# Turning the residual stream to tokens on VectorE and through DRAM instead of on TensorE

## The chip, the core and the metric

The kernel runs on one core of a Trainium2 chip. The metric is the device time of one execution in microseconds (us); the figure to be predicted is the median over several runs. The engines are named as in the profile: PE is TensorE (PEld its weight loads), DVE is VectorE, ACT is ScalarE, POOL is GpSimd and SP is SyncE, which here only issues DMAs. Each engine works through its own instructions in a fixed order and waits for others by semaphores. TensorE's granted clock is the full 2.4 GHz in nearly the whole trace.

## The reference

Two layers of a decoder trunk on 256 tokens of width 1024, in float32. Each layer adds four things to the residual stream `x`, and a last norm follows:

```
x += 1/2 SwiGLU(RMSNorm x)                       # ffn1
x += mixer(RMSNorm x)                            # layer 0: short conv | sliding-window attention; layer 1: block-sparse attention
x += MemoryCrossAttn(RMSNorm x, RMSNorm mem)
x += 1/2 SwiGLU(RMSNorm x)                       # ffn2
out = RMSNorm(x)                                 # after the last layer
SwiGLU(h) = (silu(h @ w_gate) * (h @ w_up)) @ w_down      # 1024 -> 2816 -> 1024
RMSNorm(x) = x * rsqrt(mean(x*x) + 1e-6) * g
```

## The kernel before

The stream is kept with the features on the partitions: `x` is a tile of 128 partitions by 8 feature blocks by 256 tokens. Every weight tile of 128 x 128 is loaded by SP from one long stream in DRAM, in chunks of 16 tiles (1 MB), and split into a high and a low part: ACT rounds it to `whi` (L128), DVE forms the rest `wlo` (L129). A block of 8 tiles is split at a time; splitting runs up to four blocks ahead of their use, in five buffers. For one tile TensorE does two matmuls into an accumulator (L385 with `whi` on 512 columns, L386 with `wlo` on 256). Four PSUM banks named `acc` hold accumulators.

A product of 8 such tiles makes one group: 128 features of a gate or of an up projection. When a group is done, `join` copies its PSUM bank into a `w1` tile (L395 on ACT, L396 on DVE; eight `w1` buffers). When gate and up of one `f` are both there, and the norm's factor is known, `evac` multiplies, applies silu, and splits the result for the down projection (L513, L514, L516, L453, L454).

The norm's factor may come late, since the matmuls use `x` times the gain, and the factor 1/rms per token is multiplied in afterwards. Its way is a chain over all engines. POOL squares the feature blocks and adds them up as they are made (`squares`: L325, L329, L330); for the last block ACT squares (L332, into the one `sq` buffer that POOL used) and DVE adds (L333). TensorE sums over the partitions (L354), DVE scales (L356), POOL takes the power -1/2 (L358, `rcol`), TensorE spreads the result over the partitions (L364), ACT copies it out (L366, `rbc`). Until `rbc` is there no `evac` can run; groups that finish before it wait in their `w1` tiles and then in their PSUM banks.

The last ffn differs at its end: its down projection is made with the tokens on the partitions, so that the result can be normalized and stored as it is. For that `x` must be turned as well, into `xtok` (its SBUF buffer is named `bias`). That is `to_tokens`, called 20 us into this ffn: 16 transposes on TensorE (L476), in four PSUM tiles, each copied out by ACT (L477). `xtok` is first read when the left half of the down projection is done (L571), near 938 us of the span.

The order in which an engine meets its instructions is set in two steps: a small planner in the kernel calls the pieces by due times and costs, and a scheduler of the language then orders the instructions by a simulated timeline, so an instruction that waits long in that simulation may stand later in its engine's order.

Of the kernel before, what the change touches and what calls it, by code (L numbers as in the profile page):

```python
# [15 lines left out]
F32 = mybir.dt.float32  # L16
F32R = mybir.dt.float32r
AF = mybir.ActivationFunctionType
# [5 lines left out]
P = 128  # L24
D = 1024
KT = D // P
S = 256
# [216 lines left out]
def build(nc, tc, ctx, a):  # L244
    consts = ctx.enter_context(tc.tile_pool(name="consts", bufs=1))
    wpool = ctx.enter_context(tc.tile_pool(name="wpool", bufs=1))
    act = ctx.enter_context(tc.tile_pool(name="act", bufs=1))
    psum = ctx.enter_context(tc.tile_pool(name="psum", bufs=1, space=PSUM))
    dram = ctx.enter_context(tc.tile_pool(name="dram", bufs=1, space=DRAM))
# [7 lines left out]
    def tr_tile():  # L257
        return psum.tile([P, 512], F32, name="tr", bufs=2)
# [11 lines left out]
    x = consts.tile([P, KT, S], F32, name="x")  # L270
# [8 lines left out]
    ident = consts.tile([P, P], F32, name="ident")  # L279
# [8 lines left out]
    pt = tr_tile()  # L288
# [3 lines left out]
    pe = Order()  # L292
# [175 lines left out]
            nc.vector.tensor_tensor(lo, src, hi.bitcast(F32), op=ALU.subtract)  # L468

    def to_tokens(out):  # L470
        def go():
            for u in range(2):
                for c in range(2):
                    pt = tr_tile()
                    for k in range(4):
                        nc.tensor.transpose(pt[:, k * P:(k + 1) * P], x[:, 4 * c + k, u * P:(u + 1) * P], ident)  # L476
                    nc.scalar.activation(out[:, u, c * 512:(c + 1) * 512], pt, AF.Copy)  # L477
        return go


    def ffn(which, layer, n, nxt, first=False, last=False):
# [39 lines left out]
        def down(j):  # L521
            def go():
                ps = acc_tile()
                ws.fine = j == KT - 1
                for k in range(FT):
                    w = ws.take(f"{which}_w_down", layer, k * P, j * P)
                    (mm_narrow if ws.fine else mm)(ps, w, h[k], k == 0, k == FT - 1)
                t = w1()
                part = unpaired(ps[:, :S]) if ws.fine else halves(join(t, ps))
                nc.vector.scalar_tensor_tensor(halves(t), part, 0.5, halves(n.rbc), op0=ALU.mult, op1=ALU.mult)  # L530
                add_to_x(j, halves(t), nxt)
                ws.flush()

            return always, go, FT * 327
# [66 lines left out]
        if last:  # L601
            xtok = act.tile([P, 2, D], F32, name="bias", bufs=1)
            gfin = act.tile([P, D], F32, name="kT", bufs=1)
            src = a["final_norm"]
            nc.sync.dma_start(gfin, bass.AP(tensor=src.tensor, offset=src.offset, ap=[[0, P], [1, D]]))
            pe.after(20000, to_tokens(xtok), 2000)
        pe.run(ups + (down_tok() if last else [down(j) for j in range(KT)]))


# [485 lines left out]
    pe.after(30000, biases, 0)  # L1095
    pe.after(60000, mem_scale, 0)
    ffn("ffn1", 0, n, nxt, first=True)
    bias, sinks = early["bias"], (vecs[:, VCOL["sinks"]:VCOL["sinks"] + 8], nsinks)

# [12 lines left out]
    bias = load_bias(1)  # L1112
    n, nxt = nxt, xn(("ffn1_norm", 1))
    ffn("ffn2", 0, n, nxt)
    n, nxt = nxt, xn(("mix_norm", 1))
    ffn("ffn1", 1, n, nxt)
    n, nxt = nxt, xn(("xa_norm", 1))
    odd_mixer(n, nxt, bias, mem_keys(1))
# [75 lines left out]
```

## Time and profile before

| | |
|---|---|
| median of 3 runs | 976.91 us (976.83 to 977.02) |
| the profiled execution | 975.91 us |
| its span in the profile | 974.1 us |
| PE, DVE, ACT, POOL busy | 965.1, 771.9, 599.7, 137.4 us |
| moved by DMA | 194.73 MB, 200 GB/s |

The span is the time from the first to the last instruction that the profiler shows; the execution is 1.8 us longer. Matmuls overlap each other, so a row's duration is longer than what the matmul adds to TensorE's time: that is read from the starts of neighbouring rows. Times of the rows below are from the span's start.

### The profile page before, as it was taken

To read this page: it belongs to the slowest core of one execution; us is meant where nothing else is said; L and a number is where in the kernel's file an instruction comes from. 1 tells how busy PE (TensorE), PEld (TensorE's weight loads), DVE (VectorE), ACT (ScalarE), POOL (GpSimd) and SP (SyncE) were. 2 spreads that over 40 slices of the span, in tenths; PEclk is the share of its full clock that TensorE was granted. 3 is DMA by queue.
4 is the path that set the end of the run, shared out by engine and by line. 5 is a ranking of instruction groups with operands and counts; after the bars stand their busy time and mean duration, and the time that the engine had idled before them with its cause. 6 is when DMAs were issued, how large, how long until landed. Compare 5 with 4: busy or idle time off the path is not lost.

```text
span 974.1 us, 16976 instructions
## 1 busy us (share of the span) xinstructions
PE 965.1 (99%) x6576; PEld 903.8 (93%) x6576; DVE 771.9 (79%) x1319; ACT 599.7 (62%) x1106; POOL 137.4 (14%) x149
## 2 busy tenths in 40 slices
PE   9999999999999999999999999999999999999997
PEld 8899999999999899999999999999999999999896
DVE  6989777798878987877878788777878798887663
ACT  7666655696666766665556666556784768666541
POOL 3114012201232200002300000221005050000011
PEclk9999999999999999999999999999999999999999
DMA  9896566455545666556555565565644346665631
GB/s 356 293 352 245 193 211 204 169 191 194 185 141 190 215 205 212 193 197 210 193 202 200 194 212 192 197 214 177 229 155 167 127 168 222 211 202 193 211 131 43
DMA packets 28496, 194.73 MB, mean 200 GB/s; under 512 B 3298, under 2 KB 3938, under 8 KB 5760
## 3 DMA queue, kind: packets, MB, share of 16 engines
q1 hardware_dynamic: 27072, 187.84, 55.5%
q0 software_dynamic: 912, 5.37, 1.6%
q8 instruction: 51, 0.84, 0.3%
q10 hardware_dynamic: 432, 0.44, 0.1%
q14 instruction: 29, 0.24, 0.1%
HBM read 192.57 MB, written 4.22 MB: 202 GB/s over the span
## 4 chain that ended last, share of the span: by engine, by line
PE 93%; DVE 3%; DMA 1%; ACT 1%; issue 1%; SPq 0%; POOLq 0%; DVEq 0%
PE acc L385 40%; PE acc L386 20%; PE acc L390 7%; PE acc L392 7%; PE acc L391 7%; DVE wlo L129 2%; PE acc L562 1%; PE acc L561 1%; PE acc L560 1%; DMA raw<-in_w 1%; DVE x L318 1%; PE acc L898 1%; PE acc L897 1%; PE acc L899 1%; DVE x L448 1%
## 5 line engine op out<-in xcount | busy, mean ns | idle before, releaser
L129 DVE TENSOR_TENSOR wlo<-raw,whi 128x1024 fp32r<-128x1024 f32 (+2 forms) x375 | 439.2, 1174 | 140.6 <-ACT whi L128 137.7
L128 ACT ACTIVATE whi<-raw 128x1024 fp32r<-128x1024 f32 (+2 forms) x375 | 369.7, 990 | 282.3 <-PE acc L385 134.3
L385 PE MATMUL acc<-x,whi 128*128 128x512 f32 x1392 | 458.4, 383 | 0.9 <-ACT whi L128 0.6
L386 PE MATMUL acc<-x,wlo 128*128 128x256 f32 x1392 | 378.0, 273 | 0.6 <-DVE wlo L129 0.5
L385 PEld LDWEIGHTS acc<-x,whi 128*128 128x128 f32 x1392 | 262.5, 189 | 38.4 <-ACT whi L128 1.0
L386 PEld LDWEIGHTS acc<-x,wlo 128*128 128x128 f32 x1392 | 267.3, 192 | 2.3 <-DVE wlo L129 1.5
L385 PE MATMUL acc<-h,whi 128*128 128x512 f32 x462 | 151.3, 382 | 0.0
L386 PE MATMUL acc<-h,wlo 128*128 128x256 f32 x462 | 125.4, 273 | 0.0
L385 PEld LDWEIGHTS acc<-h,whi 128*128 128x128 f32 x462 | 87.1, 189 | 12.0
L386 PEld LDWEIGHTS acc<-h,wlo 128*128 128x128 f32 x462 | 88.7, 192 | 0.2
L391 PE MATMUL acc<-h,whi 128*128 128x256 f32 x322 | 87.8, 276 | 0.0
L392 PE MATMUL acc<-h,wlo 128*128 128x256 f32 x322 | 87.7, 275 | 0.0
L390 PE MATMUL acc<-h,whi 128*128 128x256 f32 x322 | 86.5, 276 | 0.0
L391 PE MATMUL acc<-x,whi 128*128 128x256 f32 x304 | 84.1, 278 | 0.0
L392 PE MATMUL acc<-x,wlo 128*128 128x256 f32 x304 | 83.9, 277 | 0.0
L390 PE MATMUL acc<-x,whi 128*128 128x256 f32 x304 | 83.0, 277 | 0.0
L396 DVE TENSOR_TENSOR w<-acc,w 128x256 f32<-128x256 f32 x195 | 81.4, 418 | 1.1 <-ACT w L395 0.7
L395 ACT ACTIVATE w<-acc 128x256 f32<-128x256 f32 x195 | 71.8, 369 | 5.4 <-PE acc L386 5.2
L391 PEld LDWEIGHTS acc<-h,whi 128*128 128x128 f32 x322 | 61.7, 192 | 0.1
L392 PEld LDWEIGHTS acc<-h,wlo 128*128 128x128 f32 x322 | 61.7, 192 | 0.1
L390 PEld LDWEIGHTS acc<-h,whi 128*128 128x128 f32 x322 | 60.6, 192 | 0.4 <-DVE x L448 0.2
L325 POOL TENSOR_TENSOR sqacc<-x 128x256 f32<-128x256 f32 x7 | 4.3, 611 | 395.4 <-DVE x L448 395.4
(209 smaller groups left out, 1304.4 us busy)
## 6 DMA issues: line engine op xcount, KB each, us to landing
raw<-in_w SPq DMA_DIRECT2D x171, 1024.0 KB, 4.9
dists<-line POOLq DMA_DIRECT2D x2, 1536.0 KB, 12.2
raw<-in_memT SPq DMA_DIRECT2D x3, 1024.0 KB, 5.2
raw<-in_w SPq DMA_DIRECT2D x6, 384.0 KB, 6.1
bias<-dists POOLq DMA_DIRECT2D x2, 1024.0 KB, 11.4
x<-in_xT SPq DMA_DIRECT2D x1, 1024.0 KB, 7.6
out<-bias SPq DMA_DIRECT2D x2, 320.0 KB, 2.4
kT<-in_final_norm SPq DMA_DIRECT2D x1, 512.0 KB, 5.7
```

Of the source, the lines that this page charges most:

```text
L128: for ins in (self.nc.scalar.activation(hi[:, at], src, AF.Copy), self.nc.vector.tensor_tensor(lo[:, at], src, hi[:, at].bitcast(F32), op= ...
L129: self.nc.vector.tensor_tensor(lo[:, at], src, hi[:, at].bitcast(F32), op=ALU.subtract)):
L318: nc.vector.scalar_tensor_tensor(x2.lo, halves(src), g, x2.hi.bitcast(F32), op0=ALU.mult, op1=ALU.subtract)
L385: nc.tensor.matmul(ps, w[0], x2.both, start=start, stop=False)
L386: nc.tensor.matmul(ps[:, :S], w[1], x2.high, start=False, stop=stop)
L390: nc.tensor.matmul(ps[:, :S], w[0], x2.high, start=start, stop=False)
L391: nc.tensor.matmul(ps[:, :S], w[0], x2.low, start=False, stop=False)
L392: nc.tensor.matmul(ps[:, :S], w[1], x2.high, start=False, stop=stop)
L395: nc.scalar.activation(halves(out), unpaired(ps[:, S:]), AF.Copy)
L396: nc.vector.tensor_tensor(halves(out), unpaired(ps[:, :S]), halves(out), op=ALU.add)
L448: nc.vector.tensor_tensor(halves(x[:, j]), part, halves(x[:, j]), op=ALU.add)
L560: nc.tensor.matmul(ps, hh, wh, start=f == 0, stop=False)
```

## The change

`to_tokens` no longer uses TensorE and ACT. For each pair of feature blocks DVE turns a tile of 128 x 512 in blocks of 32 by 32 (a block stays at its place, only its inside is transposed). The result goes to DRAM in eight DMAs issued by POOL, each 32 partitions by 256 elements, 32 KB, written as 256 runs of 32 floats (128 bytes), so that the blocks come to their places in an array `tok` of 256 tokens by 1024 features. That makes 32 DMAs of this kind. One more DMA, also on POOL's queue, reads `tok` back into `xtok`. The turned tiles are named `q2` and have two buffers.

```diff
     def to_tokens(out):
-        def go():
-            for u in range(2):
-                for c in range(2):
-                    pt = tr_tile()
-                    for k in range(4):
-                        nc.tensor.transpose(pt[:, k * P:(k + 1) * P], x[:, 4 * c + k, u * P:(u + 1) * P], ident)
-                    nc.scalar.activation(out[:, u, c * 512:(c + 1) * 512], pt, AF.Copy)
-        return go
+        tok = dram.tile([S, D], F32, name="tok")
+        to = tok.rearrange("(c i) (k p j) -> p k i c j", i=32, p=4, j=32)
+        for k in range(0, KT, 2):
+            t = act.tile([P, 2 * S], F32, name="q2", bufs=2)
+            nc.vector.transpose(t, x[:, k:k + 2].rearrange("p k s -> p (k s)"))
+            for p in range(4):
+                for i in range(2):
+                    nc.gpsimd.dma_start(to[p, k + i], t[32 * p:32 * p + 32, i * S:(i + 1) * S].rearrange("i (c j) -> i c j", j=32))
+        nc.gpsimd.dma_start(out, tok.rearrange("(u q) f -> q u f", u=2))
...
-            pe.after(20000, to_tokens(xtok), 2000)
+            pe.after(20000, lambda: to_tokens(xtok), 0)
```

In the changed kernel the lines behind `to_tokens` have numbers three higher; the DVE transposes are L477, the DMAs to `tok` L480, the one back L481.

The engines' orders differ only around the start of the last ffn. POOL's order before, from the squares of the sixth feature block to the norm's factor (`sq` and `sqacc` are the squares and their sum, `rcol` the factor):

```order
L329 TENSOR_TENSOR sq_9484<-x_69 128x256
L330 TENSOR_TENSOR sqacc_9427<-sqacc_9427,sq_9484 128x256
L329 TENSOR_TENSOR sq_9508<-x_69 128x256
L330 TENSOR_TENSOR sqacc_9427<-sqacc_9427,sq_9508 128x256
L329 TENSOR_TENSOR sq_9528<-x_69 128x256
L330 TENSOR_TENSOR sqacc_9427<-sqacc_9427,sq_9528 128x256
L358 TENSOR_TENSOR rcol_9586<-ms_9584,mhalf_97 128x2
```

The same engine and place in the changed kernel, from the third set of eight DMAs (the first two sets stand right above, after the first and the second square):

```order
L480 DMA tok_9795<-q2_9816 32x8x32 x8
L329 TENSOR_TENSOR sq_9462<-x_69 128x256
L480 DMA tok_9795<-q2_9826 32x8x32 x8
L330 TENSOR_TENSOR sqacc_9427<-sqacc_9427,sq_9462 128x256
L329 TENSOR_TENSOR sq_9484<-x_69 128x256
L330 TENSOR_TENSOR sqacc_9427<-sqacc_9427,sq_9484 128x256
L329 TENSOR_TENSOR sq_9508<-x_69 128x256
L330 TENSOR_TENSOR sqacc_9427<-sqacc_9427,sq_9508 128x256
L481 DMA bias_9555<-tok_9795 128x2x1024
L329 TENSOR_TENSOR sq_9528<-x_69 128x256
L330 TENSOR_TENSOR sqacc_9427<-sqacc_9427,sq_9528 128x256
L358 TENSOR_TENSOR rcol_9586<-ms_9584,mhalf_97 128x2
```

All 33 DMAs now stand between the squares, ahead of the last square and of the norm's factor. TensorE's order before, from the sums over partitions (L354) to the spreading (L364) of that norm (`acc` with a number is one group of the last ffn; 9588, 9627 and 9649 are its second, third and fourth):

```order
L354 MATMUL tr_9581<-ones_95,sqacc_9427 128x1 x2
L386 MATMUL acc_9588<-x_9549,wlo_9432 128x256
L385 MATMUL acc_9627<-x_9549,whi_9487 128x512
L386 MATMUL acc_9627<-x_9549,wlo_9488 128x256
L386 MATMUL acc_9649<-x_9481,wlo_9532 128x256
L385 MATMUL acc_9649<-x_9505,whi_9531 128x512
L386 MATMUL acc_9649<-x_9505,wlo_9532 128x256
L385 MATMUL acc_9649<-x_9525,whi_9531 128x512
L386 MATMUL acc_9649<-x_9525,wlo_9532 128x256
L385 MATMUL acc_9649<-x_9549,whi_9531 128x512
L386 MATMUL acc_9649<-x_9549,wlo_9532 128x256
L364 MATMUL tr_9608<-ident_90,rcol_9586 128x128 x2
```

The same place in the changed kernel (9915 is the twelfth group of the last ffn, 9950 its thirteenth):

```order
L386 MATMUL acc_9915<-x_9525,wlo_9789 128x256
L385 MATMUL acc_9915<-x_9549,whi_9788 128x512
L386 MATMUL acc_9915<-x_9549,wlo_9789 128x256
L354 MATMUL tr_9581<-ones_95,sqacc_9427 128x1 x2
L364 MATMUL tr_9608<-ident_90,rcol_9586 128x128 x2
L385 MATMUL acc_9950<-x_9424,whi_9881 128x512
L386 MATMUL acc_9950<-x_9424,wlo_9882 128x256
```

The sums and the spreading have moved behind the twelfth group, eight groups later, and no other work of TensorE stands between them or between the spreading and the thirteenth group.

## Rows read from the trace of the kernel before

**Rows 1.** The page, busy time, share of the span and instructions of engines

```profile
PE 965.1 (99%) x6576; PEld 903.8 (93%) x6576; DVE 771.9 (79%) x1319; ACT 599.7 (62%) x1106; POOL 137.4 (14%) x149
```

**Rows 2.** The page, chain that ended last, by engine

```profile
PE 93%; DVE 3%; DMA 1%; ACT 1%; issue 1%; SPq 0%; POOLq 0%; DVEq 0%
```

**Rows 3.** Timeline of PE, 801 to 817 us: start, duration, instructions

```profile
801.51 0.50 PE L354 MATMUL tr<-ones,sqacc 128*128 128x1 f32 x4
...
803.48 0.38 PE L364 MATMUL tr<-ident,rcol 128*128 128x128 f32 x2
...
804.09 0.48 PE L385 MATMUL acc<-x,whi 128*128 128x512 f32 x1
...
804.51 0.38 PE L385 MATMUL acc<-x,whi 128*128 128x512 f32 x1
...
804.84 0.38 PE L385 MATMUL acc<-x,whi 128*128 128x512 f32 x1
...
815.10 1.04 PE L476 MATMUL tr<-ident,x 128*128 128x128 f32 x8
815.90 0.46 PE L385 MATMUL acc<-x,whi 128*128 128x512 f32 x1
```

**Rows 4.** Timeline of POOL, 786 to 803 us

```profile
786.43 0.61 POOL L325 TENSOR_TENSOR sqacc<-x 128x256 f32<-128x256 f32 x1 [29.22 <-DVE x L448]
...
797.73 1.59 POOL L330 TENSOR_TENSOR sqacc<-sqacc,sq 128x256 f32<-128x256 f32 x1
802.28 0.70 POOL L358 TENSOR_TENSOR rcol<-ms,mhalf 128x2 f32<-128x2 f32 x1 [2.96 <-DVE ms L356]
```

**Rows 5.** Groups of POOL's instructions: busy us, mean ns, idle before

```profile
L852 POOL DMA_DIRECT2D bias<-dists x2 | 1.9, 939 | 34.4 <-PE tr L713 27.0 <-PE acc L386 7.5
L845 POOL DMA_DIRECT2D dists<-line x2 | 1.1, 546 | 1.9 <-DMA line<-kT 1.9
...
L843 POOL DMA_DIRECT2D line<-kT x1 | 0.6, 644 | 10.4 <-DVE kT L842 10.4
```

**Rows 6.** DMA issues: KB each, median us from issue to landing

```profile
dists<-line POOLq DMA_DIRECT2D x2, 1536.0 KB, 12.2
...
bias<-dists POOLq DMA_DIRECT2D x2, 1024.0 KB, 11.4
...
line<-kT POOLq DMA_DIRECT2D x1, 24.0 KB, 2.2
```

**Rows 7.** Timeline of DVE, 781 to 804 us

```profile
781.45 0.69 DVE L129 TENSOR_TENSOR wlo<-raw,whi 128x512 fp32r<-128x512 f32 x1
...
800.73 0.41 DVE L333 TENSOR_TENSOR sqacc<-sqacc,sq 128x256 f32<-128x256 f32 x1
802.04 0.16 DVE L356 TENSOR_SCALAR ms<-tr 128x2 f32<-128x2 f32 x1 [0.91 <-PE tr L354]
...
803.61 0.42 DVE L396 TENSOR_TENSOR w<-acc,w 128x256 f32<-128x256 f32 x1
```

**Rows 8.** Chain that ended last, in order of time: start, us, what

```profile
797.18 3.22 DVE wlo L129 x2
```

**Rows 9.** Timeline of ACT, 799 to 813 us

```profile
799.36 0.42 ACT L332 ACTIVATE sq<-x 128x256 f32<-128x256 f32 x1 [2.18 <-POOL sqacc L330]
...
806.24 0.40 ACT L366 ACTIVATE rbc<-tr 128x256 f32<-128x256 f32 x1
...
808.37 1.28 ACT L514 ACT_TABLE_LOAD   x1
809.66 0.72 ACT L514 ACTIVATE w<-w 128x256 f32<-128x256 f32 x2
...
811.24 0.36 ACT L395 ACTIVATE w<-acc 128x256 f32<-128x256 f32 x1
...
811.98 0.72 ACT L453 ACTIVATE h<-w 128x256 fp32r<-128x256 f32 x2
```

## The prediction

> **What bounds the kernel now.** I read the page first: TensorE is busy for 99% of the span, DVE for 79%, POOL for 14% [rows 1], and the chain that ended last runs on PE for 93% of its length [rows 2]. So what counts is whether TensorE is kept going, and what of its own work goes. POOL's low share says little: around a norm, POOL is a link in a chain that TensorE waits for. That chain is read from four timelines of the same 20 us. POOL starts the last norm's squares at 786.43 and ends its last sum at 797.73 + 1.59 = 799.32 [rows 4]; ACT squares the last block at once, at 799.36 [rows 9]; DVE adds it at 800.73 [rows 7]; TensorE sums at 801.51 and spreads the factor at 803.48 [rows 3]. TensorE loses almost nothing there, because in its order ten matmuls of the second to fourth group lie between the sums and the spreading, and behind them banks are free.
>
> **The change part by part.**
>
> *Removed from TensorE:* eight transposes take from 815.10 to 815.90, 0.10 us each [rows 3]; 16 of them are 1.6 us, all on the path. The four ACT copies go too; ACT is not the bound, so I count nothing for them.
>
> *Added on DVE:* four transposes of 128 x 512. The trace has none; the nearest row is a DVE pass of the same shape, 0.69 us [rows 7]. At nothing the term would be 0, at twice the row 2.8 us in all; I take 0.6 us each. The first two stand among the adds to `x`, where DVE itself is on the chain for stretches (two splits, 3.22 us, at 797.18 [rows 8]), so 1.2 us reach TensorE. The third and fourth stand between joins, where DVE has room; they also wait for the eight DMAs that empty their buffer. Behind them in DVE's order are weight splits and joins. By the count below those DMAs are issued about when DVE gets there, and splits lie up to four blocks ahead, so I price this at nothing; without that cover it would add the wait's length.
>
> *Moved on TensorE:* sums and spreading stand behind the twelfth group instead of among the first four. A tile's pair takes 804.84 - 804.51 = 0.33 us, a group of eight pairs 2.62 us [rows 3]. The fifth group began at 804.09 after four transposes (0.4), the spreading (0.2) and the sums (0.4) that are no longer ahead of it, so it begins near 803.1; eight groups end at 803.1 + 21.0 = 824.1, with DVE's 1.2 us at 825.3. Before, the thirteenth group began at 804.09 + 21.0 + 12 x 0.10 = 826.3.
>
> *Added on POOL, ahead of the norm's factor:* 33 DMA issues. In the changed order they stand between the squares; the last square, hence the factor, is behind all of them. POOL's own DMAs cost 0.546 us (128 plain rows), 0.644 us (24 KB in a three-dimensional pattern) and 0.939 us (1024 runs) per issue [rows 5]. The new ones have 256 runs in such a pattern, between the last two. I take the middle, 0.79 us, and keep 0.55 and 0.94 as ends by these rows. 32 x 0.79 = 25.3 us; the one that reads back has 256 rows and gets 0.9 us. Added to 799.32 this gives the last sum at 825.5 (818 to 830.4). Landing should not hold POOL up: a queue slot comes round after eight DMAs, 6.3 us, and 24 KB landed in 2.2 us [rows 6]; the read-back waits for all 32 but has three sums and two squares ahead of it.
>
> *The restart.* From there to the sums: ACT 0.42, DVE 0.41 [rows 9, 7] and the hand-overs, 1.3 us: 826.8, later than TensorE's own 825.3. Now the chain is bare, since nothing stands between: sums to factor done 802.28 + 0.70 - 801.51 = 1.5 us, to the spreading 0.5 [rows 3, 4], then `rbc` (0.4 from spreading to its start, 0.40 long), the table load of 1.28 that stands behind it, four silus at 0.36, one split of `h` at 0.36, the copy of the ninth group's bank 0.36 [rows 9] and its DVE add 0.42 [rows 7], because all eight `w1` tiles and all four banks are full: in sum 6.7 us, and 0.1 to TensorE. The thirteenth group begins at 826.8 + 6.8 = 833.6. The next three banks follow within a group's time each, and up to four blocks of weights lie split, so I count no second stop.
>
> *Sum:* 833.6 - 826.3 = +7.3 us (the 1.6 us saved is in both numbers: 1.2 in the second, 0.4 in the first). The profiled execution's 975.91 becomes 983.2. It lies 1.0 us under the median of the runs, 976.91, which becomes 984.2; I say 984. With the ends of the issue price: at 0.55 TensorE's own 825.3 decides and the sum is +5.8 us, 982.7; at 0.94 it is +12.1 us, 989.
>
> **The rivals.**
>
> *Landing decides, not issue.* The third set needs buffers that the first set must have left, and a slot takes its next DMA when its last one has landed. The row that speaks for it is 1 MB in 1024 runs, 11.4 us to land [rows 6]; against it, 24 KB took 2.2 us. At 11.4 us the sets go out every 11.4: the last issue near 788.4 + 3 x 11.4 + 6.3 = 828.9, landed at 840.3, then the read-back's issue and a square and a sum (0.9 + 2.3): 843.5. With 1.3 + 6.8 us the thirteenth group begins at 851.6, +25 us: 1002. DVE's fourth transpose would then wait near 807 to 817 for the second set, inside the same stop. The weight stream shares the engines meanwhile; its chunks are three ahead.
>
> *Each DMA waits for the one ahead.* If POOL were held until a DMA has landed, 32 x 2.2 us = 70 us [rows 6] would stand in POOL's order instead of 25.3, and the last sum would be at 870.6: +52 us, 1029. Against it: two DMAs of 12.2 us each had 1.9 us of idle time before both together [rows 5, 6], so the second did not wait for the first. The Trainium skill, "DMA: Bandwidth & Descriptors", section "Anatomy of one DMA — SWDGE (gpsimd) path", gives such a DMA about 2.0 us fixed plus its bytes over 436 GB/s, and says elsewhere that transfers under 64 KB are mostly overhead; 32 x 2.1 us would be an estimate of 67 us if none overlapped. By that rule, taken one by one, the time would be near this rival's; the 2.2 us row agrees with its fixed part, and the back-to-back issues show that it overlaps.
>
> *Not slower.* TensorE's 16 transposes go, DVE and POOL have idle time, and the norm's chain ends before the twelfth group does. For this the issues must cost 0.7 us or less and also the bare restart of 6.8 us must be gone, for instance because the waiting banks are emptied in another order than L516, silu and L453 come. Then only -1.6 + 1.2 us are left: 976.5; with DVE's part hidden 975.3. Against it stands TensorE's order: nothing lies between sums, spreading and the thirteenth group, and no bank is free. It decides only below 1.6 us of restart.
>
> **How the numbers follow.** The forecast (+5.8 to +12, issue-bound) gets 0.62, landing 0.24, one by one 0.06, not slower 0.05, and 0.03 is left for stops that I don't see. About 0.2% is what a measurement here can tell from no change. Faster by that takes the second form of the last rival and more, 0.02; within it 0.04; slower 0.94. The forecast's own range is 981 to 990. The range to be held 8 times in 10 starts at 980 and reaches up through most of the landing case, to 1004.
>
> **What the profile would show.** Right: no L476 on PE; POOL busy without gaps from 786 to about 825 with L480 rows of 0.6 to 0.95 us; one stop of PE near 825, of 7 to 10 us, ending at the first matmul of the thirteenth group, released by DVE's L396; nothing changed after 840 but the shift. Landing would show as idle POOL time between sets with a DMA as releaser, and a PE stop over 20 us. One by one would show such gaps before every issue. I am wrong if PE has no stop over 3 us in 800 to 850, or if a second stop, from late splits or late weight chunks, is as long as the first.

## The result and the profile after

| | before | after |
|---|---|---|
| median, lowest to highest | 976.96 us (976.83 to 978.19) | 988.40 us (987.04 to 989.28), 4 runs each |
| ratio, 95% interval | | 1.0118 (1.0105 to 1.0130) |
| the profiled execution, its span | 975.91, 974.1 us | 989.16, 987.0 us |

The change makes the kernel 11.4 us slower. The forecast was 984, so the sign and the stop were foreseen and the size was 4.4 us short.

Before the two traces are compared, one offset has to be taken out. The first square of the last norm stands at 786.43 before [rows 4] and at 788.75 after, 2.3 us later, although no changed instruction runs ahead of it. The delay is older still: the first weight load for a norm's sums stands at 27.5 us before and at 29.8 after (all instructions of one line, in the traces of before and of after: durations, then first and last start):

```profile
L354 PEld LDWEIGHTS tr<-ones,sqacc x36: 189/192/192, 27.5 to 801.7; 128*128 128x128 f32 x36
L354 PEld LDWEIGHTS tr<-ones,sqacc x36: 189/192/333, 29.8 to 831.1; 128*128 128x128 f32 x36
```

It arises in the first 9 us. TensorE waits there 2.39 us for a weight split, where it waited 0.56 us before, and that split waits 2.24 us for its weights to land, 0.36 us before. So below, "in before's time" means 2.3 us less than the trace of after shows. TensorE's page row and its timeline around the last norm (start, duration, instructions, idle time before and what ended it):

```profile
PE 966.0 (98%) x6560; PEld 903.5 (92%) x6560; DVE 771.9 (78%) x1323; ACT 598.5 (61%) x1102; POOL 156.6 (16%) x182
```

```profile
804.82 0.27 PE L386 MATMUL acc<-x,wlo 128*128 128x256 f32 x1
806.75 0.48 PE L385 MATMUL acc<-x,whi 128*128 128x512 f32 x1 [1.65 <-DVE w L396]
...
827.70 0.27 PE L386 MATMUL acc<-x,wlo 128*128 128x256 f32 x1
830.60 0.95 PE L354 MATMUL tr<-ones,sqacc 128*128 128x1 f32 x4 [2.63 <-DVE sqacc L333]
832.59 0.69 PE L364 MATMUL tr<-ident,rcol 128*128 128x128 f32 x2 [1.04 <-POOL rcol L358]
837.71 0.77 PE L385 MATMUL acc<-x,whi 128*128 128x512 f32 x1 [4.43 <-DVE w L396]
...
838.48 0.63 PE L385 MATMUL acc<-x,whi 128*128 128x512 f32 x1
...
841.00 0.38 PE L385 MATMUL acc<-x,whi 128*128 128x512 f32 x1
...
841.32 0.38 PE L385 MATMUL acc<-x,whi 128*128 128x512 f32 x1
```

Where TensorE went on without a gap before [rows 3], it now stops twice: 1.65 us ahead of the fifth group, and from the end of the twelfth group, 827.97, to the thirteenth at 837.71, a gap of 9.7 us with 0.6 us of necessary work in it. And it comes out of the gap slowly: a tile's pair takes 0.64 us from 838.48 on, twice the 0.33 of before, until 841.00. The stretches around it say why (columns: the stretch, its length, busy time of five engines, granted TensorE clock, DMA share, GB/s):

```profile
824.00:828.00 4.00, 3.97 (x25) 3.39 (x23) 2.20 (x2) 1.16 (x2) 2.15 (x3) 1.00 0.86 317
828.00:832.00 4.00, 0.95 (x4) 0.86 (x4) 1.72 (x3) 1.26 (x2) 0.17 (x1) 0.84 0.99 387
832.00:836.00 4.00, 0.69 (x2) 0.29 (x2) 2.14 (x7) 2.65 (x6) 0.54 (x1) 0.50 0.13 53
836.00:840.00 4.00, 2.29 (x7) 2.05 (x8) 4.00 (x13) 3.07 (x11) 0.00 (x0) 0.50 0.00 0
840.00:844.00 4.00, 4.00 (x23) 3.58 (x23) 2.60 (x6) 2.50 (x5) 0.00 (x0) 0.88 0.00 0
```

With TensorE busy for only 0.95 and 0.69 us of two stretches, its granted clock fell from 1.00 to 0.50, that is to 1.2 GHz. From 837.71 to 841.00 five pairs take 3.29 us; at full clock five such pairs took 0.42 + 4 x 0.33 = 1.74 [rows 3]. That costs 1.55, rounded 1.6 us.

POOL, the engine on which the forecast let the stop depend, first with its timeline, then with all DMAs to `tok` in one row (durations in ns, least, median and most) and their landing:

```profile
788.75 0.61 POOL L325 TENSOR_TENSOR sqacc<-x 128x256 f32<-128x256 f32 x1 [29.22 <-DVE x L448]
...
802.97 4.62 POOL L480 DMA_DIRECT2D tok<-q  x8 [1.20 <-DVE q L477]
...
813.56 4.64 POOL L480 DMA_DIRECT2D tok<-q  x8 [5.26 <-DVE q L477]
...
823.79 0.76 POOL L481 DMA_DIRECT2D bias<-tok  x1
...
825.52 0.73 POOL L330 TENSOR_TENSOR sqacc<-sqacc,sq 128x256 f32<-128x256 f32 x1
```

```profile
L480 POOL DMA_DIRECT2D tok<-q x32: 585/585/642, 790.7 to 817.6; - x32
...
DMA to landing us min/median/max: 1.9/3.2/6.0
```

POOL ends its last sum at 825.52 + 0.73 = 826.25. The sums on TensorE start 4.35 us later. What lies between is on ACT and DVE:

```profile
804.04 1.06 ACT L128 ACTIVATE whi<-raw 128x1024 fp32r<-128x1024 f32 x1 [4.54 <-PE acc L385]
...
827.90 1.06 ACT L128 ACTIVATE whi<-raw 128x1024 fp32r<-128x1024 f32 x1 [1.56 <-PE acc L385]
828.86 0.40 ACT L332 ACTIVATE sq<-x 128x256 f32<-128x256 f32 x1
833.32 0.38 ACT L366 ACTIVATE rbc<-tr 128x256 f32<-128x256 f32 x1 [4.06 <-PE tr L364]
833.72 1.28 ACT L517 ACT_TABLE_LOAD   x1
```

```profile
801.97 0.70 DVE L477 STREAM_TRANSPOSE q<-x 128x512 f32<-128x512 f32 x1
...
828.99 1.23 DVE L129 TENSOR_TENSOR wlo<-raw,whi 128x1024 fp32r<-128x1024 f32 x1 [1.39 <-ACT whi L128]
830.13 0.42 DVE L333 TENSOR_TENSOR sqacc<-sqacc,sq 128x256 f32<-128x256 f32 x1
...
837.15 0.42 DVE L396 TENSOR_TENSOR w<-acc,w 128x256 f32<-128x256 f32 x1
```

The last square (L332) and its sum (L333) stand on their engines behind one block's weight split (L128, L129). That split waits until TensorE, at the end of the twelfth group, lets go of a split buffer. So the norm's last step waits for the very group behind which TensorE then waits for the norm.

In the trace of before the thirteenth group began here:

```profile
826.46 0.38 PE L385 MATMUL acc<-x,whi 128*128 128x512 f32 x1
```

In before's time the step is: thirteenth group at 835.4 against 826.5, +8.9 us; half clock, +1.6; together 10.5. The spans differ by 12.9, without the late start by 10.6.

### The profile page after: what moved, and what is told of

Read it like the earlier page. It is cut to its first block, busy times and chain, and to the rows that moved or that the text cites. A ratio compares the mean times of both kernels' runs of the same rounds, so it can differ in the third digit from the quotient of the medians.

```text
span 987.0 us, 16987 instructions
## 1 busy us (share of the span) xinstructions
PE 966.0 (98%) x6560; PEld 903.5 (92%) x6560; DVE 771.9 (78%) x1323; ACT 598.5 (61%) x1102; POOL 156.6 (16%) x182
## 4 chain that ended last, share of the span: by engine, by line
PE 94%; DVE 2%; ACT 1%; issue 1%; DMA 1%; POOL 0%; SPq 0%; POOLq 0%; DVEq 0%
PE acc L385 40%; PE acc L386 20%; PE acc L392 7%; PE acc L390 7%; PE acc L391 7%; PE acc L565 1%; PE acc L564 1%; PE acc L563 1%; DVE wlo L129 1%; PE acc L901 1%; PE acc L902 1%; PE acc L900 1%; DMA raw<-in_w 1%; ACT whi L128 0%; PE sc L563 0%
## 5 line engine op out<-in xcount | busy, mean ns | idle before, releaser
L129 DVE TENSOR_TENSOR wlo<-raw,whi 128x1024 fp32r<-128x1024 f32 (+2 forms) x375 | 437.0, 1168 | 152.0 <-ACT whi L128 146.8
L128 ACT ACTIVATE whi<-raw 128x1024 fp32r<-128x1024 f32 (+2 forms) x375 | 369.5, 989 | 293.9 <-PE acc L385 148.2
L385 PEld LDWEIGHTS acc<-h,whi 128*128 128x128 f32 x462 | 87.1, 189 | 12.0
L396 DVE TENSOR_TENSOR w<-acc,w 128x256 f32<-128x256 f32 x195 | 81.3, 417 | 1.1 <-ACT w L395 0.7
L391 PEld LDWEIGHTS acc<-h,whi 128*128 128x128 f32 x322 | 61.7, 192 | 0.1
L329 POOL TENSOR_TENSOR sq<-x 128x256 f32<-128x256 f32 x42 | 47.4, 1128 | 88.3 <-DVE x L448 87.2
## 6 DMA issues: line engine op xcount, KB each, us to landing
bias<-dists POOLq DMA_DIRECT2D x2, 1024.0 KB, 11.4
```

What stands on the lines that cost most here:

```text
L128: for ins in (self.nc.scalar.activation(hi[:, at], src, AF.Copy), self.nc.vector.tensor_tensor(lo[:, at], src, hi[:, at].bitcast(F32), op= ...
L129: self.nc.vector.tensor_tensor(lo[:, at], src, hi[:, at].bitcast(F32), op=ALU.subtract)):
L329: nc.gpsimd.tensor_tensor(sq, src, src, op=ALU.mult)
L385: nc.tensor.matmul(ps, w[0], x2.both, start=start, stop=False)
L391: nc.tensor.matmul(ps[:, :S], w[0], x2.low, start=False, stop=False)
L396: nc.vector.tensor_tensor(halves(out), unpaired(ps[:, :S]), halves(out), op=ALU.add)
```

## The experiments

Three theories. A: the loss is made by the place at which sums and spreading stand in TensorE's order; behind the twelfth group nothing covers the norm's chain, whatever POOL's real pace. B: POOL's time for the DMA issues is the loss, since the factor is late by as much as POOL is busy. C: DVE's transposes, and the waits for their two buffers, are the loss. Each kernel is compared with runs of the kernel before on the same chip: their median was 976.09 us (26 runs) for the first four kernels and 976.43 (9 runs) for the other four.

**The turning behind the factor.** Each turned tile first takes a column of the factor, so nothing of the turning can come ahead of the norm. The same transposes and DMAs are made, and one small copy on POOL for each tile.

```diff
-    def to_tokens(out):
+    def to_tokens(out, n):
...
             t = act.tile([P, 2 * S], F32, name="q2", bufs=2)
+            nc.gpsimd.tensor_copy(t[:, :1], n.rcol[:, :1])
             nc.vector.transpose(t, x[:, k:k + 2].rearrange("p k s -> p (k s)"))
```

> All of the change, but each turned tile first gets one element from the norm's factor, so that transposes and DMAs come behind the factor on DVE and POOL; sums and spreading are back among the first four groups in TensorE's order. Theory A (the place of the sums in TensorE's order makes the stop): no stop near 825, 975 to 976 us, the 1.6 us of TensorE's transposes gained less what DVE gives back. Theory B (POOL's time for the DMA issues makes the factor late): the same, since the issues are behind the factor. Theory C (the four transposes and their waits for buffers take DVE from the splits and joins): still slower than before, 979 us or more.

Measured: 974.75 us (974.30 to 975.67), ratio to before 0.9985 (0.9976 to 0.9994). TensorE's sums stand at 801.75 and its spreading at 803.72, as before. The waits of TensorE and of POOL from 784 to 870 us, one row of each (waiter, releaser, us in total, times, longest):

```profile
PE acc L385 <- DVE w L396: 0.2, 1, 0.2
```

```profile
POOL tok L481 <- DVE q L478: 12.3, 3, 5.7
```

All added work is still there, POOL even waits 12.3 us for DVE, and 1.3 us are gained: TensorE's 1.6 for the transposes less 0.2 of a wait. So neither the transposes nor the waits for their buffers cost much where they stand behind the factor; C among the adds to `x` is left to the third experiment. This is the version that beats both kernels.

**The DMAs from SP.** The order of issue is kept, but POOL is freed of it.

```diff
-                    nc.gpsimd.dma_start(to[p, k + i], ...)
-        nc.gpsimd.dma_start(out, ...)
+                    nc.sync.dma_start(to[p, k + i], ...)
+        nc.sync.dma_start(out, ...)
```

> All of the change, but the 33 DMAs are issued by SP instead of POOL, at the same early place; the first two DVE transposes stay among the adds to x. In TensorE's order the sums stand behind the fourth group and the spreading behind the fifth. A: the long stop is gone, 976 to 978 us. B: the same or less, 975 to 977. C: 980 us or more, since the transposes are where they were. A risk outside all three: weight loads stand behind the 32 issues in SP's queue; if they come late, PE waits for splits with a DMA as releaser, some us.

Measured: 976.43 us (976.01 to 978.03), ratio 1.0003 (0.9994 to 1.0012): no difference from before. The sums now stand behind the fourth group and the spreading behind the fifth; TensorE's timeline there:

```profile
803.70 0.50 PE L354 MATMUL tr<-ones,sqacc 128*128 128x1 f32 x4
805.51 0.48 PE L385 MATMUL acc<-x,whi 128*128 128x512 f32 x1 [1.31 <-DVE w L396]
...
808.24 0.38 PE L364 MATMUL tr<-ident,rcol 128*128 128x128 f32 x2
```

The 10 us are gone with POOL's issues; 1.3 us of stop, and 0.3 elsewhere, stay and eat the 1.6 us of the transposes. But this run takes away both POOL's time and the late place, so A and B are not yet told apart.

**DVE's transposes alone.** The kernel before, with the four DVE transposes added and read by nobody; TensorE's transposes stay.

```diff
+    def turn_only():
+        for k in range(0, KT, 2):
+            t = act.tile([P, 2 * S], F32, name="q2", bufs=2)
+            nc.vector.transpose(t, x[:, k:k + 2].rearrange("p k s -> p (k s)"))
...
+            pe.after(20000, turn_only, 0)
             pe.after(20000, to_tokens(xtok), 2000)
```

> The kernel before, with its TensorE transposes, and the four DVE transposes added whose tiles nobody reads; no new DMA. Sums stand behind the fourth group, spreading behind the fifth. A and B: 977 to 979 us, 1 to 2 us for the first two transposes that stand among the adds. C: most of the loss, 983 us or more.

Measured: 978.57 us (977.86 to 979.58), ratio 1.0023 (1.0014 to 1.0033), +2.2 us by the ratio and +2.5 by the medians. TensorE waits 1.3 us for L396 ahead of the fifth group, like the SP kernel, and twice 0.3. So the four transposes, with the order that they bring about, cost 2 to 2.5 us, of which the forecast had 1.2, and C does not make the 11 us.

**The DMAs alone.** The kernel before, with 32 DMAs of the same pattern on POOL, straight from `x` to an array that nobody reads; no DVE transposes and no read-back, and TensorE's transposes stay.

```diff
+    def copy_only():
+        tok = dram.tile([S, D], F32, name="tok")
+        to = tok.rearrange("(c i) (k p j) -> p k i c j", i=32, p=4, j=32)
+        for k in range(0, KT, 2):
+            for p in range(4):
+                for i in range(2):
+                    nc.gpsimd.dma_start(to[p, k + i], x[32 * p:32 * p + 32, k + i].rearrange("i (c j) -> i c j", j=32))
...
+            pe.after(20000, copy_only, 0)
             pe.after(20000, to_tokens(xtok), 2000)
```

> The kernel before, with its TensorE transposes, and the 32 DMAs on POOL straight from x to an array that nobody reads (no DVE transposes, no read-back). In TensorE's order sums and spreading stand behind the twelfth group, as in the changed kernel. A: the same stop, 9 to 11 us at half clock behind it, 985 to 988 us. B: POOL has no waits for DVE here and needs no read-back, its last sum comes 6 to 7 us earlier than in the changed kernel, so the loss should shrink by as much, 980 to 982. C: 977.

Measured: 987.01 us (986.36 to 987.62), ratio 1.0109 (1.0095 to 1.0122). POOL, which never waits for DVE here, then DVE and TensorE:

```profile
796.34 2.88 POOL L486 DMA_DIRECT2D tok<-x  x5 [0.79 <-DMA tok<-x]
...
820.15 0.73 POOL L330 TENSOR_TENSOR sqacc<-sqacc,sq 128x256 f32<-128x256 f32 x1
828.42 0.71 POOL L358 TENSOR_TENSOR rcol<-ms,mhalf 128x2 f32<-128x2 f32 x1 [7.54 <-DVE ms L356]
```

```profile
825.92 1.22 DVE L129 TENSOR_TENSOR wlo<-raw,whi 128x1024 fp32r<-128x1024 f32 x1 [1.39 <-ACT whi L128]
827.06 0.42 DVE L333 TENSOR_TENSOR sqacc<-sqacc,sq 128x256 f32<-128x256 f32 x1
```

```profile
824.63 0.27 PE L386 MATMUL acc<-x,wlo 128*128 128x256 f32 x1
827.53 0.61 PE L354 MATMUL tr<-ones,sqacc 128*128 128x1 f32 x4 [2.63 <-DVE sqacc L333]
...
834.23 0.66 PE L476 MATMUL tr<-ident,x 128*128 128x128 f32 x4 [1.84 <-ACT bias L477]
835.66 0.80 PE L385 MATMUL acc<-x,whi 128*128 128x512 f32 x1 [0.78 <-DVE w L396]
```

This run tells A from B. POOL is done at 820.88, 4.0 us before the twelfth group ends at 824.90, and TensorE still waits 2.63 us for L333, to the hundredth as in the changed kernel, and again begins the thirteenth group only at 835.7. The square and its sum wait for the split behind the twelfth group, not for POOL. The stop is there without a single DVE transpose.

**The changed kernel once more.** Unchanged, beside the three kernels that follow.

> The changed kernel itself again, beside the next three on one chip and in more runs: its profiled run began its first layer 2.3 us later than that of before, which the change has no part in. If that was this one run's start, the median here lies 10.5 to 11 us above before, 986.5 to 987.5; if the start is always late, 988 or more.

Measured: 987.38 us (986.40 to 988.62), ratio 1.0113 (1.0099 to 1.0127), +10.95 us. The profiled execution, 988.62, shows the same stops (1.65, 2.63, 1.05 and 4.43 us) and a start 1.5 us late (its first square of the last norm at 787.91). Without their late starts the two profiled executions of this kernel would take 986.9 and 987.1 us. One thing differs: seven slow pairs follow the stop here, from the first row to the second, and not five.

```profile
836.53 0.77 PE L385 MATMUL acc<-x,whi 128*128 128x512 f32 x1 [4.43 <-DVE w L396]
...
841.14 0.38 PE L385 MATMUL acc<-x,whi 128*128 128x512 f32 x1
```

They take 4.61 us; seven at full clock would take 0.42 + 6 x 0.33 = 2.40, so the clock cost 2.2 us in this execution.

**The stop filled.** Matmuls with zeros keep TensorE at work in the stop: 10 into the open accumulator of the twelfth group, 16 into the spreading's bank once `rbc` is copied out.

```diff
             nc.scalar.activation(n.rbc, pt[:, :S], AF.Copy)
+            if n.last:
+                for _ in range(16):
+                    nc.tensor.matmul(pt[:, :P], warm, warm, start=True, stop=True)
...
+                if last and f == 5 and part == 1 and ks[-1] == KT - 1:
+                    for i in range(10):
+                        nc.tensor.matmul(ps[:, :P], warm, warm, start=False, stop=i == 9)
...
```

> The changed kernel with TensorE work of no use put into its stop: 10 matmuls of a zero tile into the open accumulator of the twelfth group ahead of the sums (about 2.3 us), 16 into the spread factor's PSUM tile once it is read (about 3.8 us). Nothing waits less. If the half clock behind the stop costs the 1.6 us that its slow matmuls show (five tile pairs of 0.64 us instead of 0.33), the time falls by 1 to 2 us against the changed kernel on this chip; if the stop alone is the price, it stays within 0.4 us; if the filling is itself late, it rises by 1 or more.

Measured: 985.89 us (985.58 to 986.52), ratio to before 1.0098 (1.0084 to 1.0111). TensorE, with a start 0.1 us late, and the stretches:

```profile
828.36 0.61 PE L355 MATMUL tr<-ones,sqacc 128*128 128x1 f32 x4 [0.40 <-DVE sqacc L334]
...
830.92 5.46 PE L370 MATMUL tr<-warm 128*128 128x128 f32 x32 [0.47 <-ACT rbc L367]
836.14 0.46 PE L389 MATMUL acc<-x,whi 128*128 128x512 f32 x1
```

```profile
832.00:836.00 4.00, 4.00 (x24) 4.00 (x23) 3.70 (x12) 3.80 (x13) 0.00 (x0) 0.57 0.00 0
836.00:840.00 4.00, 4.00 (x27) 3.71 (x26) 2.92 (x9) 2.65 (x6) 0.00 (x0) 1.00 0.00 0
```

From 836 on the clock is full and every pair takes 0.33 us. The fillers, at 0.57 of the clock for most of their time, overran the end of the chain, so the thirteenth group begins 0.7 us later than in the changed kernel in before's time (836.1 against 835.4). Between the profiled executions without late starts the gain is 1.3 us or a little more (986.9 and 987.1 against 985.6), between the medians 1.5. By the rows, 1.6 to 2.2 us of slow pairs less these 0.7 us make 0.9 to 1.5. The two intervals of the ratios overlap, so the size of the clock's term rests on the slow pairs; this run shows that with work inside the stop the pairs behind it are not slow.

**Every DMA twice.** Each DMA is issued a second time into an array that nobody reads: 64 issues instead of 32.

```diff
+        to_b = dram.tile([S, D], F32, name="tok_b").rearrange("(c i) (k p j) -> p k i c j", i=32, p=4, j=32)
...
+                    nc.gpsimd.dma_start(to_b[p, k + i], t[32 * p:32 * p + 32, i * S:(i + 1) * S].rearrange("i (c j) -> i c j", j=32))
                     nc.gpsimd.dma_start(to[p, k + i], t[32 * p:32 * p + 32, i * S:(i + 1) * S].rearrange("i (c j) -> i c j", j=32))
```

> The changed kernel with each of the 32 DMAs issued twice (the second copy to an array that nobody reads), so 32 more issues of 0.585 us = 18.7 us on POOL ahead of the norm's factor. TensorE's order is the same: sums and spreading behind the twelfth group. Theory A with POOL's slack of 3 to 4 us (its last sum stood at 826.25, what DVE added to it at 830.13): 18.7 - 3.5 = 15 us more, near 1002. Theory B (POOL's time always decides): the full 18.7 us or more, 1006 and up. If POOL's time had no part at all: 988.

Measured: 1001.33 us (1001.14 to 1002.66), ratio to before 1.0259 (1.0244 to 1.0275), 13.95 us more than the changed kernel beside it. POOL, DVE and TensorE:

```profile
840.93 0.72 POOL L330 TENSOR_TENSOR sqacc<-sqacc,sq 128x256 f32<-128x256 f32 x1
```

```profile
842.13 0.42 DVE L333 TENSOR_TENSOR sqacc<-sqacc,sq 128x256 f32<-128x256 f32 x1 [14.73 <-ACT sq L332]
```

```profile
842.61 1.01 PE L354 MATMUL tr<-ones,sqacc 128*128 128x1 f32 x4 [17.45 <-DVE sqacc L333]
...
849.78 0.76 PE L385 MATMUL acc<-x,whi 128*128 128x512 f32 x1 [4.43 <-DVE w L396]
```

Here B's mechanism works: POOL ends at 841.65 and DVE's L333 follows 0.48 us later. In the changed kernel L333 began 830.13 - 826.25 = 3.88 us behind POOL's end, so POOL had 3.88 - 0.48 = 3.4 us of slack there. This trace starts 0.2 us early (first square at 786.20), so in before's time POOL's end moved from 823.9 to 841.9, by 18.0 us; 18.0 - 3.4 = 14.6. The thirteenth group moved by as much, from 835.4 to 850.0, and the median by 13.95. So POOL's pace counts only beyond that slack, and in the changed kernel it did not decide. The restart is the same, 842.61 to 849.78, 7.2 us.

**Half the DMAs.** The DMAs-alone kernel with 16 instead of 32.

```diff
-        for k in range(0, KT, 2):
+        for k in range(0, KT // 2, 2):
```

> As the run with the DMAs alone, but only 16 of them. In TensorE's order the sums now stand in the middle of the tenth group and the spreading in the twelfth, with ten tile pairs between them and some six pairs and 16 transposes behind, ahead of the thirteenth group. A: the bare chain is mostly covered again, a stop of 1 to 3 us, 978 to 980 us. B: half of the DMAs, half of the loss, 981 to 983.

Measured: 979.73 us (979.44 to 981.38), ratio 1.0038 (1.0025 to 1.0050). The sums stand in the middle of the tenth group, at 818.36, and the spreading in the twelfth, at 823.07, both without a wait. TensorE stops 1.07 us at 803.63, 1.81 at its transposes and 0.85 at 830.16, 3.7 us together. POOL's last sum ends at 811.97, 6.4 us ahead of TensorE's sums. Between 16 and 32 DMAs the price goes from 3.3 us to 10.9, though POOL's issues are merely doubled and in neither run do TensorE's sums wait for POOL. By the rows the step is the loss of the groups that lay between sums, spreading and the next use.

Taken together, by the place of sums and spreading: among the second to fourth groups -1.3 us (turning behind the factor, against its before), behind the fourth and fifth +0.3 (SP), in the tenth and twelfth +3.3 (16 DMAs), both behind the twelfth +10.9 (32 DMAs) and +10.95 (the changed kernel). The first two go without TensorE's 16 transposes, worth 1.6 us, and the third still has them, as the DMAs-alone kernel has.

## Why the prediction was short by 4.4 us

| step | forecast | measured, in before's time |
|---|---|---|
| fifth group begins | 804.3 | 804.4 |
| twelfth group ends | 825.3 | 825.7 |
| POOL's last sum ends | 825.5 | 823.9 |
| sums over partitions begin | 826.8 | 828.3 |
| from there to the thirteenth group | 6.8 | 7.1 |
| thirteenth group begins, against before (826.3 in the forecast, 826.5 in the trace) | +7.3 | +8.9 |
| half clock behind it | not counted | +1.6 |

*Right.* TensorE's order decided it, and the bare restart behind the twelfth group was sized to 0.3 us (7.1, and 7.2 with the DMAs doubled). The forecast's 1.2 us for DVE's transposes met a stop of 1.65 us ahead of the fifth group: the transposes took 0.70 us each instead of 0.6, and the ACT split that stands ahead of the first group's join waited 4.54 us for TensorE. Only part of that stop is the transposes' own, since the DMAs-alone kernel, without them, stops there for 0.88 us too; that the fifth group's begin fits to 0.1 us is partly luck. Of the signs, the stop near 825 came and ended at L396 as written, but POOL was not busy without gaps. The read-back from `tok` landed 7.4 us after its issue, long before 938 us, and stopped nothing.

*The step that failed* is the one from "the last sum at 825.5" to the sums: "ACT 0.42, DVE 0.41 [rows 9, 7] and the hand-overs, 1.3 us: 826.8". It took POOL for the last to arrive and let the last square follow at once. Measured, POOL was 1.6 us earlier than forecast, and the square was not free to follow: split L128 and L129 stood ahead of it and waited for the end of the twelfth group. The sums were 2.63 us behind that end and not 1.5. With POOL's measured end, the forecast's own sum would have been TensorE's 825.3 and +5.8 us, further off. What was missing is a look at what stands ahead of L332 and L333 on their engines: I counted POOL's queue to the instruction and took ACT and DVE as free.

*Two errors that cancelled* lie inside POOL's term. An issue was priced at 0.79 us, between two POOL rows [rows 5], and took 0.585: 32 x 0.205 = 6.6 us too much. The waits for DVE's third and fourth transposes were priced at nothing on the path; they held POOL for 1.20 + 5.26 = 6.5 us. POOL's own squares and sums ran 1.4 us shorter than before, which leaves the 1.6 us. The 6.5 us cost nothing in the end, but only because POOL had slack.

*Not in the sum:* the clock. A stop of 7 to 10 us was forecast, and nothing was put down for the pace behind it. The slow pairs show 1.6 us, and 2.2 in the repeat.

*The rivals.* Landing did not decide: the DMAs landed in 3.2 us at the median, and the only idle time of POOL between issues that no DVE transpose ended is 0.15 us. That a slot comes round after eight does show in the DMAs-alone kernel: the thirteenth issue, at 796.34, waited 0.79 us for the landing of the fifth, issued at 790.93. One by one is refuted by eight issues in 4.62 us without a gap. The Trainium skill, "DMA: Bandwidth & Descriptors", section "Anatomy of one DMA — SWDGE (gpsimd) path", puts the fixed part of such a DMA at about 2.0 us. With its term for the bytes, that gives an estimate of 2.1 us for 32 KB. The quickest of the 32, 1.9, agrees with the fixed part; the median of 3.2, beside the weight stream, lies above the estimate. "Not slower" needed the restart gone, and that is what the first experiment does: with the factor ahead of the turning, 974.75 us, where that rival was priced at 975.3 to 976.5.

*What stays open.* Of the +11.4 us by the medians (+10.95 in the repeat), 10.5 are accounted for, with the repeat's seven slow pairs some 0.6 more. The rest is of the size of the late starts, 2.3 and 1.5 us in the two profiled executions of this kernel and 0.1 to 0.3 in those of the DMAs alone and of the filled stop. Most of a late start is a wait for the first weights, as shown above; why they land later in some executions was not tried. No run moved the last square alone ahead of the split, so that the 2.63 us would go with it is read from the rows and not shown. That the scheduler's simulated timeline moved the sums because of POOL's DMAs is inferred from the orders of these kernels (0, 16, 32 and 64 DMAs on POOL ahead of the factor); the timeline itself was not seen.

## What to carry to other kernels

Work added to an idle engine can cost by the order it brings about, not by its time: a side task put ahead of a link of a critical chain moved that chain behind its last cover, and making the task depend on the end of the chain turned +11 us into -1.3 us. When a chain over several engines is timed, ask on each of them what stands ahead of the link and what that waits for; here it waited for the group that was to be covered. A long stop of TensorE can cost more than its length: five to seven pairs ran at half the clock behind the stop of 9.7 us, and none behind that of 1.65 us.

## What the runs showed of the hardware

- POOL's issue of a DMA of 32 KB in 256 runs of 128 bytes took 0.585 us (0.642 at most), less than the 0.644 of the 24 KB pattern [rows 5], and as much when 64 of them were issued. From SP the same issues had a median of 0.448 us (0.302 to 1.651), and landing took 2.6 us instead of 3.2.
- A DVE transpose of 128 x 512 float32 in blocks of 32 by 32 took 0.70 us, as long as a pass of the same shape, 0.69 [rows 7].
- After 9.7 us with about 1.6 us of busy time on TensorE, the granted clock stood at 0.50, and the first five tile pairs (seven in the repeat) took 0.64 us each instead of 0.33. With fillers in the stop the clock stood at 1.00 from the first pair on, but the last 5.46 us of fillers ran for most of their time at half of it (0.57 in the mean of 832 to 836).
